# Weight conversions of an MLP's up stage tied to the relu, with a split first load and a reordered last norm

## The chip, the cores and the metric

The kernel runs on one core of a Trainium2 chip, as one launch. The metric is the device time of an execution in microseconds. The engines have short names here: PE (TensorE), DVE (VectorE), ACT (ScalarE), POOL (GpSimd) and SP (the queue that issues most DMAs).

## The reference

A decoder trunk of two layers on 512 tokens of width 1024, all in float32. Layer 0 is a gated short convolution, layer 1 a native sparse attention; each is followed by the same kind of MLP. The MLP is what most of this change is about.

```python
def rms_norm(x, g):
    y = x * lax.rsqrt(jnp.mean(x * x, axis=-1, keepdims=True) + EPS)
    return y * g

def squared_relu_mlp(h, w1, w2):              # w1 (1024, 4096), w2 (4096, 1024)
    return jnp.square(jax.nn.relu(h @ w1)) @ w2

def reference(x, ...):
    for layer in range(2):
        h = rms_norm(x, norm_mix[layer])
        x = x + (short_conv_mixer(h, ...) if layer == 0 else nsa_mixer(h, ..., shared, rel_bias))
        x = x + squared_relu_mlp(rms_norm(x, norm_mlp[layer]), mlp_w1[layer], mlp_w2[layer])
        if layer == 0:
            shared = nsa_shared_kv(rms_norm(x, kv_norm), ...)
    return rms_norm(x, final_norm)
```

## The kernel before

Products are made in float16 with three matmuls each (`mm3`): a float32 operand is split into a high half `hi` (ACT) and the remainder `lo` (DVE), and hi·hi, hi·lo and lo·hi are summed in PSUM. So every weight must be loaded (SP), then converted: `whi` by ACT and `wlo` by DVE. The weights are a list `pieces` in the order of use. Each has one of two kinds.

- An ordinary piece is [128, 1024] float32. Its tile is `wst` (`NS` = 3 buffers), its halves are `whi` and `wlo` (`NW` = 4).
- A block piece belongs to the down product. That product is made with seven block products instead of eight (a Strassen-Winograd scheme): DVE first adds four sums of 256-element blocks to the piece (line 180), then ACT writes `whi2` (line 182) and DVE `wlo2` (line 183), 1792 wide. There are three buffers for loading (`NS2`) and four for the halves (`NW2`), in the memory of the stage's own pool, so they can't be loaded before that pool opens.

`load_piece` issues the DMAs of the next piece, `convert_piece` converts the next one and loads another, `next_piece` hands the next one to a product, and `ahead` converts up to two ordinary pieces (`AHEAD`) or three block pieces (`AHEAD2`) ahead of use. One position in the list serves both kinds for each of these steps.

The program is written in a framework that places the instructions of each engine by a simulated schedule: an instruction may stand in its queue ahead of those that the text has before it, if its inputs are ready sooner. `tc.issue_after(ins)` keeps what is written in its block behind `ins` in the queue of the engine of `ins`, and does not bind other engines.

Each MLP runs in two halves of the hidden width: `mlp_up` on eight pairs of hidden tiles (p = 0 to 7), `mlp_down` on the result. A pair takes two pieces and 48 matmuls into two of six PSUM banks (lines 339 to 341). Then for each p: DVE scales and clips (`ml_t`, line 497), ACT squares (`ml_z`, 499), POOL adds four block sums (501), ACT writes `rh` (502) and DVE `rl` (503). `mlp_down` goes over four column blocks p; in each it runs over eight hidden tiles c with 21 matmuls each (lines 548 to 550), a block piece for two tiles. `ss.rstd` (lines 296 to 303) computes the reciprocal root of the norm ahead, during the first pair, and `broadcast_rows` (310) turns it into a row on PE.

The start: `x` comes in column chunks; PE transposes chunk c (line 372), ACT and DVE write its halves `x0h`, `x0l` with the norm's gain `vec`, which itself is a PE transpose (277) and two ACT copies (278, 279). `keep_busy` issues matmuls on zeros (237). The first eight weight pieces hold the three parts B, C and u of the mixer's input product side by side, 256 columns each.

The end: `last_b` finishes the last column block. Its combine steps are on DVE (1168), PE turns the result to token order (1121), ACT sums squares (1117), DVE multiplies by the gains (1192, 1198), and `store` computes the reciprocal root for two token tiles, scales them on ACT and DVE (1150 to 1157) and stores them (1158).

Of the kernel before, what the change touches and what calls it, by code (L numbers as in the profile page):

```python
# [48 lines left out]
def body(ctx, tc, x, rel_bias, norm_mix, norm_mlp, mlp_w1, mlp_w2, a_w_in, a_conv_w, a_w_out,  # L49
         kv_norm, w_kv, cmp_pe_k, cmp_pe_v, phi_k_w1, phi_k_w2, phi_v_w1, phi_v_w2,  # L50
         b_w_qg, b_w_o, final_norm, ident_c, onehot_c, out):
    nc = tc.nc
# [84 lines left out]
    W_SUMS = ((OP.add, 4, 0, 2), (OP.subtract, 5, 4, 1), (OP.subtract, 6, 1, 0), (OP.subtract, 7, 3, 5))  # L137
    R_SUMS = ((OP.subtract, 4, 0, 1), (OP.subtract, 5, 2, 4), (OP.subtract, 6, 2, 0), (OP.subtract, 7, 3, 5))

    PRODUCTS = ((1, 1), (3, 3), (5, 5), (6, 6), (4, 4), (7, 2), (2, 7))  # L140
    staged, ready = {}, {}
    pos = {"dma": 0, "cv": 0, "use": 0}
# [4 lines left out]
    def load_piece():  # L147
        i = pos["dma"]
        if i >= len(pieces):
            return  # L150
# [16 lines left out]
        pos["dma"] += 1  # L167

    def convert_piece(step=1024):

        i = pos["cv"]
        if i >= len(pieces):
            return
        _, shape, sc = pieces[i]
        t = staged.pop(i)
        pos["cv"] += 1
        if shape is None:
            b = t.rearrange("p (k b n) -> p k b n", k=2, n=128)
            for e, o, x, y in W_SUMS:
                DVE.tensor_tensor(b[:, :, o], b[:, :, x], b[:, :, y], op=e)  # L180
# [5 lines left out]
        else:  # L186
# [3 lines left out]
            for s in range(0, a * n, step):  # L190
                e = min(s + step, a * n)
                w = t[:, s:e]
                ACT.activation(hi[:, s:e], w, AF.Copy, scale=sc)  # L193
                DVE.scalar_tensor_tensor(lo[:, s:e], w, sc, hi[:, s:e], op0=OP.mult, op1=OP.subtract)  # L194
# [3 lines left out]
        while pos["dma"] < len(pieces):  # L198
            like = [j for j in range(pos["cv"], pos["dma"]) if blocked(j) == blocked(pos["dma"])]
            if len(like) >= (NS2 if blocked(pos["dma"]) else NS):  # L200
                break
            load_piece()

    def next_piece():

        i = pos["use"]
        pos["use"] += 1
        while i not in ready:
            for _ in convert_piece():
                pass  # L210
# [66 lines left out]
    PE.transpose(pv[:, 0:64], vec_in, ident[0:64, 0:64])  # L277
# [13 lines left out]

    def rstd_of(ss):
# [3 lines left out]
        ACT.activation(r, ss, AF.Sqrt, bias=eps, scale=1.0 / D)  # L296
# [46 lines left out]
    def pair(xs, ps, kn=8, mid=None):  # L343

        for c in range(kn):
            if c % 4 == 0:
                if c:
# [21 lines left out]
    def x_chunk(c):  # L369
# [3 lines left out]
        if c == 0:  # L373
            with tc.issue_after(last.ins):
# [110 lines left out]
    def mlp_up(xs, ss, rh, half, rb):  # L485
        turn[0] = 1
        for p in range(8):
            ph = [acc(), acc()]
            first = p == 0 and half == 0
            pair(xs, ph, mid=ss.rstd if first else None)  # L490
# [3 lines left out]
            drain(ahead())  # L494
            t = wk[0].tile([128, 2, S], F32, name="ml_t", bufs=1)
            for m in range(2):
                DVE.scalar_tensor_tensor(t[:, m], ph[m], 0.0, rb, op0=OP.max, op1=OP.mult)  # L497
# [76 lines left out]
    def first_half(hp, xs, ss):  # L574
        rh = tuple(hp.tile([128, 8, 7, 256], F16, name=n) for n in ("rh", "rl"))
# [22 lines left out]
    with pool("attn") as ap:  # L598
# [70 lines left out]
        def ahead_fine():  # L669
            while pos["cv"] < min(pos["use"] + AHEAD, len(pieces)):  # L670
                yield from convert_piece(512)
# [428 lines left out]
    with pool("hidden_b") as hp:  # L1100
# [42 lines left out]
        def store(h, late=None):  # L1143
            sst = work.tile([128, 2], F32, name="sst", bufs=2)
            DVE.tensor_reduce(sst, ssf[:, 2 * h:2 * h + 2], axis=mybir.AxisListType.X, op=OP.add)
            r = rstd_of(sst)
            for i in range(2):
                t = 2 * h + i
                a, b = xt[t][:, 0:512], xt[t][:, 512:1024]
                ACT.activation(a, a, AF.Copy, scale=r[:, i:i + 1])  # L1150
                if late:
                    b = xt[t][:, 512:768]
                    DVE.scalar_tensor_tensor(xt[t][:, 768:896], late[i], r[:, i:i + 1], gains(3, 1),
                                             op0=OP.mult, op1=OP.mult)
                    c = xt[t][:, 896:1024]
                    DVE.tensor_scalar(c, c, r[:, i:i + 1], None, op0=OP.mult)
                DVE.tensor_scalar(b, b, r[:, i:i + 1], None, op0=OP.mult)
                nc.sync.dma_start(out[0, t * 128:(t + 1) * 128, :], xt[t])

        def last_b(acc7, product):  # L1160
# [26 lines left out]
            stt(X1[:, n1], P2, X1[:, n1])  # L1187
            for t in range(2):
# [3 lines left out]
                DVE.tensor_tensor(xt[t][:, 768:1024], ps[:, 0:256], gains(3), op=OP.mult)  # L1192
            store(0)
            for t in range(2, 4):
# [3 lines left out]
                DVE.tensor_tensor(xt[t][:, 896:1024], ps[:, 0:128], gains(3)[:, 128:256], op=OP.mult)  # L1198
            product(6)
            stt(X2[:, n1], P4, X2[:, n1])  # L1200
# [6 lines left out]
            store(1, late)  # L1207
# [31 lines left out]
```

## Time and profile before

| what | value |
|---|---|
| timed runs | 1150.41, 1153.44, 1153.8 us; median 1153.44 |
| profiled execution | 1151.28 us, span 1149.5 us |
| mean granted PE clock | 0.994 |
| busy: PE, DVE, ACT, POOL | 1106.0, 837.8, 582.7, 162.2 us |
| DMA | 115.76 MB, mean 101 GB/s |

In a line of the timeline stand start, duration, engine, line of the kernel, operation, written and read tiles with shapes, and count; in brackets the idle time of the engine ahead of it and what ended it. A line of the waits has total, times and longest. A line of the stretches has the busy time of PE, PE's weight load, DVE, ACT and POOL, each with the number of instructions, then granted clock, DMA share and GB/s. Matmuls overlap; a 512-wide one is shown as 0.38 us and a 256-wide one as 0.27 us, whatever the distance to the next.

### The profile page before, as it was taken

The numbers are of one execution on the slowest core, as the hardware profiler recorded it, in microseconds if no ns is written. First come the engines' busy times: TensorE is split into PE (matmuls) and PEld (weight loads), VectorE is DVE, ScalarE is ACT, GpSimd is POOL, SyncE is SP. The second block draws the span as 40 slices with busy tenths as digits, with TensorE's granted clock in tenths as the row PEclk, the third lists the DMA queues.
The fourth block names the chain that finished last, engine by engine and source line by source line (L and its number), as shares of the span: only waits on it lengthen the run. The fifth ranks groups of instructions, "written<-read, shape, count | busy, mean of one in ns | idle before, by whom it ended". The sixth has DMA issues, their size and how long they took to land.

```text
span 1149.5 us, 20386 instructions
## 1 busy us (share of the span) xinstructions
PE 1106.0 (96%) x7959; PEld 694.1 (60%) x7959; DVE 837.8 (73%) x1604; ACT 582.7 (51%) x983; POOL 162.2 (14%) x211
## 2 busy tenths in 40 slices
PE   9999999999999999999999899999999999999996
PEld 4444444447884458868466665765444688445885
DVE  4755557765897557988487898997985588754795
ACT  4523235345333444457679778676644534343452
POOL 0000000422000220000120023111132200022031
PEclk9999999999999999999999999999999999999998
DMA  6433235433433333314333530111643343330231
GB/s 208 130 92 110 92 111 174 119 93 93 127 98 108 109 110 107 97 55 122 110 79 99 143 94 19 57 38 38 186 126 99 88 126 110 104 99 19 75 92 74
DMA packets 149379, 115.76 MB, mean 101 GB/s; under 512 B 8612, under 2 KB 146564, under 8 KB 149284
## 3 DMA queue, kind: packets, MB, share of 16 engines
q1 hardware_dynamic: 146736, 109.47, 31.8%
q10 hardware_dynamic: 2260, 4.40, 1.3%
q8 instruction: 62, 1.02, 0.4%
q0 software_dynamic: 288, 0.61, 0.2%
q14 instruction: 33, 0.27, 0.1%
HBM read 110.22 MB, written 2.14 MB: 98 GB/s over the span
## 4 chain that ended last, share of the span: by engine, by line
PE 49%; DVE 20%; ACT 12%; issue 8%; POOL 6%; DMA 4%; SPq 0%; DVEq 0%; ACTq 0%; POOLq 0%
POOL ml_z L501 6%; PE a L340 4%; PE a L339 4%; PE a L341 4%; DVE wlo L183 4%; DMA wst<-mlp_w_dram 4%; ACT rh L502 3%; PE b L339 3%; PE b L340 3%; PE b L341 3%; PE c L341 3%; PE c L339 3%; PE c L340 3%; DVE wst L180 3%; DVE wlo L194 3%
## 5 line engine op out<-in xcount | busy, mean ns | idle before, releaser
L193 ACT ACTIVATE whi<-wst 128x1024 f16<-128x1024 f32 (+2 forms) x171 | 142.2, 857 | 128.3 <-PE b L340 40.0
L194 DVE SCALAR_TENSOR_TENSOR wlo<-wst,whi 128x1024 f16<-128x1024 f32 (+2 forms) x171 | 168.1, 990 | 47.3 <-ACT whi L193 47.1
L501 POOL TENSOR_TENSOR ml_z<-ml_z 128x256 f32<-128x256 f32 x128 | 101.1, 811 | 604.5 <-ACT ml_z L499 403.9
L182 ACT ACTIVATE whi<-wst 128x1792 f16<-128x1792 f32 x64 | 107.0, 1692 | 132.6 <-DVE wst L180 107.8
L341 PEld LDWEIGHTS <-wlo 128*128 128x128 f16 x1024 | 100.1, 98 | 109.3 <-DVE wlo L194 0.7
L339 PEld LDWEIGHTS <-whi 128*128 128x128 f16 x1024 | 100.4, 98 | 108.1 <-issue 3.7
L503 DVE TENSOR_TENSOR rl<-ml_z,rh 128x1792 f16<-128x1792 f32 x32 | 64.8, 2025 | 136.9 <-ACT rh L502 136.9
L340 PEld LDWEIGHTS <-whi 128*128 128x128 f16 x1024 | 100.2, 98 | 105.0 <-issue 1.7
L183 DVE SCALAR_TENSOR_TENSOR wlo<-wst,whi 128x1792 f16<-128x1792 f32 x64 | 129.8, 2033 | 3.6 <-ACT whi L182 3.6
L180 DVE TENSOR_TENSOR wst<-wst 128x256 f32<-128x256 f32 x256 | 105.9, 455 | 24.1 <-DMA wst<-mlp_w_dram 23.1
L502 ACT ACTIVATE rh<-ml_z 128x1792 f16<-128x1792 f32 x32 | 54.3, 1697 | 103.4 <-POOL ml_z L501 103.4
L550 PEld LDWEIGHTS <-wlo 128*128 128x128 f16 x896 | 88.1, 98 | 16.6 <-issue 5.1
L549 PEld LDWEIGHTS <-whi 128*128 128x128 f16 x896 | 88.1, 98 | 14.8 <-issue 3.9
L548 PEld LDWEIGHTS <-whi 128*128 128x128 f16 x896 | 88.2, 98 | 11.0
L499 ACT ACTIVATE ml_z<-ml_t 128x1024 f32<-128x1024 f32 x32 | 33.8, 1057 | 90.5 <-DVE ml_t L497 90.5
L341 PE MATMUL b<-xsh,wlo 128*128 128x512 f16 x208 | 78.8, 379 | 0.0
L340 PE MATMUL b<-xsl,whi 128*128 128x512 f16 x208 | 78.8, 379 | 0.0
L339 PE MATMUL b<-xsh,whi 128*128 128x512 f16 x208 | 78.7, 379 | 0.0
L922 ACT ACTIVATE at_p<-at_s,at_m 128x128 f32<-128x128 f32 (+3 forms) x128 | 71.3, 557 | 13.4 <-DVE at_m L919 13.0
L549 PE MATMUL a<-rl,whi 128*128 128x256 f16 x256 | 70.3, 275 | 4.6 <-DVE rl L503 4.6
L339 PE MATMUL c<-xsh,whi 128*128 128x512 f16 x192 | 72.8, 379 | 0.0
L340 PE MATMUL c<-xsl,whi 128*128 128x512 f16 x192 | 72.8, 379 | 0.0
(312 smaller groups left out, 2757.5 us busy)
## 6 DMA issues: line engine op xcount, KB each, us to landing
wst<-mlp_w_dram SPq DMA_DIRECT2D x256, 256.0 KB, 3.4
wst<-a_w_in_dram SPq DMA_DIRECT2D x18, 512.0 KB, 3.6
wst<-w_kv_dram SPq DMA_DIRECT2D x12, 512.0 KB, 3.7
T<-ext_d ACTq DMA_DIRECT2D x4, 1056.0 KB, 6.0
wst<-a_w_out_dram SPq DMA_DIRECT2D x8, 512.0 KB, 3.5
wst<-b_w_qg_dram SPq DMA_DIRECT2D x8, 512.0 KB, 4.3
wst<-b_w_o_dram SPq DMA_DIRECT2D x8, 512.0 KB, 3.5
wst<-a_w_in_dram SPq DMA_DIRECT2D x8, 384.0 KB, 5.5
```

The source lines that it names most:

```text
L180: DVE.tensor_tensor(b[:, :, o], b[:, :, x], b[:, :, y], op=e)
L182: ACT.activation(hi, b[:, :, 1:], AF.Copy, scale=sc)
L183: DVE.scalar_tensor_tensor(lo, b[:, :, 1:], sc, hi, op0=OP.mult, op1=OP.subtract)
L193: ACT.activation(hi[:, s:e], w, AF.Copy, scale=sc)
L194: DVE.scalar_tensor_tensor(lo[:, s:e], w, sc, hi[:, s:e], op0=OP.mult, op1=OP.subtract)
L339: PE.matmul(ps, w[0], xs[0], start=start, stop=False)
L340: PE.matmul(ps, w[0], xs[1], start=False, stop=False)
L341: PE.matmul(ps, w[1], xs[0], start=False, stop=stop)
L501: POOL.tensor_tensor(z[:, o], z[:, a], z[:, b], op=e)
L502: ACT.activation(rh[0][:, p], z[:, 1:8], AF.Copy)
L548: PE.matmul(acc7[i], wh, xh, start=c == 0 and not other, stop=False, skip_group_check=other)
L549: PE.matmul(acc7[i], wh, xl, start=False, stop=False, skip_group_check=other)
```

## The change

1. The one list position becomes one queue for each kind (`to_load`, `to_convert`), with `fill(kind)` to load as long as buffers are free; `layer_end` keeps block pieces of the next layer out.
2. In `mlp_up` the products no longer call `ahead`. At p = 0 block pieces begin to load and two ordinary pieces are converted. Behind the scaled relu (`issue_after(done.ins)`) come two ordinary pieces for p below 6, and one block piece for p = 1 to 4.
3. Two of the four block sums become one instruction over two blocks.
4. The first piece is loaded and converted in three parts, and the idle matmuls of the start are put behind the turn of `vec` as well.
5. In the last norm the gain multiplies and both reciprocal roots go behind the last combine step; token tile 0 is scaled on POOL, tile 1 on ACT, and the stores stand in the order 0, 2, 3, 1.

```diff
-    def load_piece():
-        i = pos["dma"]
...
+    def load_piece(kind=False):
+        i = to_load[kind].pop(0)
...
+            elif i == 0:
+                for part in FIRST_PARTS:
+                    nc.sync.dma_start(v[:, part], src[:, part])
...
+    def fill(kind):
+        while (to_load[kind] and sum(blocked(j) == kind for j in staged) < (NS2 if kind else NS)
+               and not (kind and to_load[kind][0] > layer_end[0])):
+            load_piece(kind)
...
-            for e, o, x, y in W_SUMS:
-                DVE.tensor_tensor(b[:, :, o], b[:, :, x], b[:, :, y], op=e)
+            DVE.tensor_tensor(b[:, :, 4], b[:, :, 0], b[:, :, 2], op=OP.add)
+            DVE.tensor_tensor(b[:, :, 5:7], b[:, :, 4:0:-3], b[:, :, 1::-1], op=OP.subtract)
+            DVE.tensor_tensor(b[:, :, 7], b[:, :, 3], b[:, :, 5], op=OP.subtract)
...
+            if i == 0:
+                spans = [(n * part, n * part + n) for part in FIRST_PARTS]
...
     def ahead():
-        while pos["cv"] < len(pieces) and pos["cv"] < pos["use"] + (AHEAD2 if blocked(pos["cv"]) else AHEAD):
-            yield from convert_piece()
+        for kind in (False, True):
+            while to_convert[kind] and to_convert[kind][0] < use[0] + (AHEAD2 if kind else AHEAD):
+                yield from convert_piece(kind)
...
-            with tc.issue_after(last.ins):
+            with tc.issue_after(last.ins), tc.issue_after(vec_turn.ins):
                 keep_busy(5)
...
-            pair(xs, ph, mid=ss.rstd if first else None)
+            pair(xs, ph, mid=ss.rstd if first else None, convert=False)
...
-            drain(ahead())
+            if p == 0:
+                fill(True)
+                for _ in range(2):
+                    drain(convert_piece(False))
...
-                DVE.scalar_tensor_tensor(t[:, m], ph[m], 0.0, rb, op0=OP.max, op1=OP.mult)
+                done = DVE.scalar_tensor_tensor(t[:, m], ph[m], 0.0, rb, op0=OP.max, op1=OP.mult)
+
+            with tc.issue_after(done.ins):
+                if p < 6:
+                    for _ in range(2):
+                        drain(convert_piece(False))
+                if 1 <= p < 5:
+                    drain(convert_piece(True))
...
     def first_half(hp, xs, ss):
+        layer_end[0] = use[0] + 63
...
-            store(1, late)
+            with tc.issue_after(final.ins):
+                for t, ps, at, g in early:
+                    DVE.tensor_tensor(xt[t][:, at], ps, g, op=OP.mult)
+                r = stats(0)
+                lo, hi = slice(0, 512), slice(512, 1024)
+                for at in (lo, hi):
+                    v = xt[0][:, at]
+                    POOL.tensor_tensor(v, v, r[:, 0:1].to_broadcast([128, 512]), op=OP.mult)
+                put(0)
+                r1 = stats(1)
+            with tc.issue_after(rstd_root[0].ins):
+                ACT.activation(xt[1][:, lo], xt[1][:, lo], AF.Copy, scale=r[:, 1:2])
+                for i in range(2):
+                    v = xt[2 + i][:, lo]
+                    ACT.activation(v, v, AF.Copy, scale=r1[:, i:i + 1])
+                    DVE.scalar_tensor_tensor(xt[2 + i][:, 768:896], late[i], r1[:, i:i + 1], gains(3, 1),
+                                             op0=OP.mult, op1=OP.mult)
+                    v = xt[2 + i][:, 896:1024]
+                    DVE.tensor_scalar(v, v, r1[:, i:i + 1], None, op0=OP.mult)
+                    v = xt[2 + i][:, 512:768]
+                    DVE.tensor_scalar(v, v, r1[:, i:i + 1], None, op0=OP.mult)
+                    put(2 + i)
+                ACT.activation(xt[1][:, hi], xt[1][:, hi], AF.Copy, scale=r[:, 1:2])
+                put(1)
```

`final` is the last combine step (line 1168 before), `stats` returns the reciprocal root of two token tiles, `put(t)` stores one, and `rstd_root[0]` is the latest square root on ACT.

More of the change, by code (lines that the diff above doesn't have):

```diff
@@ L276, in body @@
     pv = bank("e")
[L277 removed]
+    vec_turn = PE.transpose(pv[:, 0:64], vec_in, ident[0:64, 0:64])
     ACT.activation(vec[:, 0:40], pv[:, 0:40], AF.Copy, scale=SX)
@@ L669, in ahead_fine @@
         def ahead_fine():
-            while pos["cv"] < min(pos["use"] + AHEAD, len(pieces)):
-                yield from convert_piece(512)
+            while to_convert[False] and to_convert[False][0] < use[0] + AHEAD:
+                yield from convert_piece(False, 512)
         def keys(br):
@@ L1141, in done_b, with stats, put @@
             yield
-        def store(h, late=None):
+        def stats(h):
             sst = work.tile([128, 2], F32, name="sst", bufs=2)
             DVE.tensor_reduce(sst, ssf[:, 2 * h:2 * h + 2], axis=mybir.AxisListType.X, op=OP.add)
[L1146 to L1158, printed above, removed]
+            return rstd_of(sst)
+        def put(t):
+            nc.sync.dma_start(out[0, t * 128:(t + 1) * 128, :], xt[t])
         def last_b(acc7, product):
@@ L1191, in last_b @@
                 square(ps[:, 0:256], t, 3)
-                DVE.tensor_tensor(xt[t][:, 768:1024], ps[:, 0:256], gains(3), op=OP.mult)
-            store(0)
+                early.append((t, ps[:, 0:256], slice(768, 1024), gains(3)))
             for t in range(2, 4):
```

47 lines of the change are left out of this document (21 added, 26 removed).

## The prediction

> **What bounds the kernel now.** I read the engine totals first, then what the matmul queue waited for, then the timeline of the few places found.
>
> ```profile
> PE 1106.0 (96%) x7959; PEld 694.1 (60%) x7959; DVE 837.8 (73%) x1604; ACT 582.7 (51%) x983; POOL 162.2 (14%) x211
> ...
> 855.00:885.00 30.00, 30.00 (x140) 13.50 (x139) 18.66 (x22) 13.63 (x12) 10.40 (x12) 1.00 0.36 105
> ```
>
> TensorE is the bound. Inside the up stage it never rests: 140 matmuls in 30.00 us are 0.214 us each, so one pair (48 matmuls) takes 10.3 us. A change that removes no matmul can give back only pauses, half-clock time and the two ends. The waits of TensorE say which pauses belong to the MLP stages and the tail:
>
> ```profile
> PE a L549 <- DVE rl L503: 4.6, 3, 1.8
> PE e L310 <- DVE rs_r L303: 1.8, 2, 1.4
> PE c L1121 <- DVE X L1168: 1.4, 1, 1.4
> PE a L548 <- ACT rh L502: 1.0, 1, 1.0
> ...
> 284.85 0.27 PE L549 MATMUL a<-rl,whi 128*128 128x256 f16 x1 [1.55 <-DVE rl L503]
> 442.48 0.27 PE L549 MATMUL a<-rl,whi 128*128 128x256 f16 x1 [1.23 <-DVE rl L503]
> 913.78 0.27 PE L548 MATMUL a<-rh,whi 128*128 128x256 f16 x1 [1.05 <-ACT rh L502]
> 915.84 0.37 PE L549 MATMUL a<-rl,whi 128*128 128x256 f16 x1 [1.79 <-DVE rl L503]
> ...
> 915.90:921.60 5.70, 5.70 (x28) 4.04 (x28) 3.76 (x2) 2.85 (x3) 0.00 (x0) 0.50 0.34 99
> 921.60:930.00 8.40, 8.40 (x78) 7.49 (x77) 8.17 (x14) 1.70 (x1) 0.00 (x0) 0.99 0.39 123
> ```
>
> Three of the four up halves end in a pause: the down stage has used seven of the eight hidden tiles and waits for the last one's `rh`/`rl`. After the third pause the granted clock is 0.50 for 5.7 us: 28 matmuls where 53 would have fitted (78 in 8.40 us are 0.108 each).
>
> Why the last `rl` is late is in the DVE queue of the same half:
>
> ```profile
> 265.47 1.28 DVE L497 SCALAR_TENSOR_TENSOR ml_t<-b,rb 128x512 f32<-128x512 f32 x2
> 266.67 1.21 DVE L194 SCALAR_TENSOR_TENSOR wlo<-wst,whi 128x1024 f16<-128x1024 f32 x1
> 272.58 2.02 DVE L503 TENSOR_TENSOR rl<-ml_z,rh 128x1792 f16<-128x1792 f32 x1 [4.70 <-ACT rh L502]
> 274.52 1.22 DVE L194 SCALAR_TENSOR_TENSOR wlo<-wst,whi 128x1024 f16<-128x1024 f32 x1
> 275.66 1.28 DVE L497 SCALAR_TENSOR_TENSOR ml_t<-c,rb 128x512 f32<-128x512 f32 x2
> 282.77 2.03 DVE L503 TENSOR_TENSOR rl<-ml_z,rh 128x1792 f16<-128x1792 f32 x1 [4.70 <-ACT rh L502]
> ```
>
> This is a serial loop: relu, square on ACT, four sums on POOL, `rh` on ACT, `rl` on DVE, a weight's `wlo`, next relu. It turns in 10.19 us (265.47 to 275.66), hardly faster than the 10.3 us of a pair, so a lag once caught is never made up. PSUM holds three pairs, so TensorE runs ahead and pays only at the end. The lag is caught early, when block sums and their `wlo` are run greedily:
>
> ```profile
> 211.11 1.28 DVE L497 SCALAR_TENSOR_TENSOR ml_t<-c,rb 128x512 f32<-128x512 f32 x2
> 212.31 1.21 DVE L194 SCALAR_TENSOR_TENSOR wlo<-wst,whi 128x1024 f16<-128x1024 f32 x1
> 213.44 2.02 DVE L183 SCALAR_TENSOR_TENSOR wlo<-wst,whi 128x1792 f16<-128x1792 f32 x1
> 215.37 2.68 DVE L180 TENSOR_TENSOR wst<-wst 128x256 f32<-128x256 f32 x3
> 220.40 2.02 DVE L503 TENSOR_TENSOR rl<-ml_z,rh 128x1792 f16<-128x1792 f32 x1 [2.35 <-ACT rh L502]
> ...
> 224.15 1.28 DVE L497 SCALAR_TENSOR_TENSOR ml_t<-a,rb 128x512 f32<-128x512 f32 x2
> ```
>
> That turn took 13.04 us.
>
> **The change, part by part.** The sum is made against the profiled execution, 1151.28 us (span 1149.5 and 1.8 around it). The timed runs are 1150.41, 1153.44 and 1153.8; the mean of all four is 1152.2, and I put the saving on that.
>
> *Pins in the up stage.* No work is removed. After each relu come two `wlo` of the pair two ahead (p below 6) and, for p = 1 to 4, one block piece; for p = 6 and 7 nothing. So `rl` is followed directly by the next relu. A turn without a block becomes 10.19 - 1.14 (274.52 to 275.66) = 9.05 us, 1.25 under a pair: lag is now made up. A turn with a block is nearest to the row of 211.11: relu to the end of `rl` is 9.29 + 1.94 = 11.2 us, with one `wlo`, one block `wlo` and three sums inside and 2.35 us idle, which takes the second `wlo` (1.13) and the fourth sum. So 0.9 us over a pair, 3.6 us after four, made up by p = 7. The last `rl` then ends about 9 us after the last up matmul, while seven hidden tiles (147 matmuls of 0.108, 15.9 us) cover it. If that cover were short, the old pauses return. All three pauses go. The idle figures start at a modelled end, 0.27 after the start, where the pace is 0.108, so each stands for 0.16 more: 5.62 + 0.64 = 6.26 us, and the half clock 5.70 - 28 x 0.108 = 2.7 us. Together 8.9 us; bounds 3 (only the lag of the third half goes) and 9.
>
> One rule of the Trainium skill bears on the 2.7 us: "TensorE: Matmul & The Clock Gate", Part 1, has the clock halved only after an idle window of about 3.4 us. By that rule of the Trainium skill pauses of 1.05 and 1.79 us would not have done it; the rows show 0.50 right behind them, and I go by the rows.
>
> *Waits that are added.* Behind a pinned `wlo` in DVE's queue wait block sums, `rl` and the next relu. TensorE needs the `wlo` of pair p+2 when that pair starts, 10.3 us after pair p; they end 1.2 + 2 x 1.2 = 3.6 us after the relu begins. The cover is 6.7 us of lag.
>
> *Loads.* Two queues of pieces replace one, and SP gets the first three block loads at p = 0.
>
> ```profile
> wst<-mlp_w_dram SPq DMA_DIRECT2D x256, 256.0 KB, 3.4
> ```
>
> What is queued behind them on SP are the up pieces, two DMAs each; three are staged and two are used per 10.3 us, so 3.4 us to landing leaves slack of about 3 us behind `wlo`. I cost this at nothing, up to 3 us once if the cover is gone.
>
> *The norm before the up stage.*
>
> ```profile
> 191.32 0.17 DVE L299 RECIPROCAL rs_r<-rs_r 128x4 f32<-128x4 f32 x1
> 191.40 1.99 DVE L183 SCALAR_TENSOR_TENSOR wlo<-wst,whi 128x1792 f16<-128x1792 f32 x1
> 193.31 0.15 DVE L301 TENSOR_TENSOR rs_t<-rs_r 128x4 f32<-128x4 f32 x1
> 194.20 1.08 DVE L180 TENSOR_TENSOR wst<-wst 128x256 f32<-128x256 f32 x3
> ```
>
> A block's `wlo` and two sums sit inside the chain of the reciprocal root. With block pieces pinned behind p = 1 they cannot. The two waits (1.8 us above) go: 1.7 us, bounds 0 (an up `wlo` takes the place) and 2.
>
> *Two sums in one.* Three 256-element sums take 1.08 us, 0.34 each; two 512-element relus start 0.60 apart. So 2 x 0.34 - 0.60 = 0.08 us per piece, 5 us over 64 pieces, all beside TensorE: 0 on the path, bounds 0 and -0.6.
>
> *First piece by parts; idle matmuls behind the gain turn.*
>
> ```profile
> 5.67 1.89 PE L237 MATMUL c<-idle 128*128 128x512 f16 x5
> 7.49 0.28 PE L277 MATMUL e<-ident,vec_in 64*128 64x64 f32 x1
> 8.45 0.66 PE L372 MATMUL e<-ident,xt 128*128 128x128 f32 x4 [0.68 <-ACT vec L279]
> 9.09 0.38 PE L339 MATMUL a<-x0h,whi 128*128 128x512 f16 x1
> ```
>
> The turn moves ahead of five idle matmuls (1.8 us), so the gains and the first `x0h` come that much sooner, and a third of the piece lands and converts first. If the first product still follows chunk 1's transposes, which wait for that chunk's load, 0.3 us is won; if not, it starts at about 7.7, 1.4 us sooner. I take 0.8.
>
> *Last norm.*
>
> ```profile
> 1138.16 0.27 PE L550 MATMUL e<-rh,wlo 128*128 128x256 f16 x1
> ...
> 1139.42 0.40 DVE L1168 SCALAR_TENSOR_TENSOR X<-e,X 128x256 f32<-128x256 f32 x1
> 1141.31 0.96 SPq L1158 DMA_DIRECT2D out_dram<-xsh  x2
> 1144.37 1.05 SPq L1158 DMA_DIRECT2D out_dram<-xsl  x2
> ...
> 1142.20:1144.60 2.40, 0.00 (x0) 0.00 (x0) 2.07 (x11) 1.33 (x3) 0.00 (x0) 0.79 1.00 399
> out_dram<-xsl SPq DMA_DIRECT2D x2, 512.0 KB, 2.9
> L739 POOL TENSOR_TENSOR Q<-at_s,Q 64x512 f16<-64x512 f32 x16 | 19.2, 1197 | 72.7 <-ACT Q L738 71.8
> ```
>
> The last combine step can start at about 1138.5 instead of 1139.42: 0.9 us. But tiles 0 and 1, stored from 1141.31 until now, wait for work that is put behind it, and all four stores come in one bunch. A store is 0.52 MB, 1.3 us at 399 GB/s, and the row of 2.9 us leaves 1.6 us around that. Before, the last bunch of two landed at about 1144.37 + 1.6 + 2.6 = 1148.6. After, the first store is the question. If a tile of the second pair goes first: 1144.37 stands 4.95 us behind the combine step, from 1138.5 that is 1143.4, less one 512-wide scaling on ACT that no longer stands ahead of the squares, about 1142.7 (an estimate). If tile 0 goes first and the others queue behind it on SP: the gain multiplies that are now behind the step hold the first root until about 1141.5, and POOL's two multiplies at 1.2 us each, with some contention, end near 1144.2. With 1.6 + 5.2 us behind it the last landing is 1149.5 or 1151.0: a loss of 0.9 to 2.4 us. I take 1.5.
>
> Sum: -8.9 - 1.7 - 0.8 + 1.5 = -9.9 us: 1152.2 - 9.9 = 1142.3 (1141.4 beside the profiled execution).
>
> **Rivals.**
> *The pauses come back elsewhere* (the last hidden tile stays late, or the scheduled order hardly differs, so that the change does not do what it says). For: the loop through ACT and POOL stays. Against: the fourth half has no such wait and no pause. Then only 1.0 us is left: 1151.2.
>
> *The clock drop is not the pause's.* Then the 2.7 us stay: 1145.0. For it: the clock rule of the Trainium skill named above. Against: the two shorter pauses kept the clock, this pair lost it.
>
> *DVE's loop becomes the bound, the slower side.* Place: turns p = 1 to 4 of each half. It decides from a turn of 10.3 + 6.7/4 = 12.0 us, where the `wlo` of pair p+2 come late. At the 13.04 us measured above, 4 x 2.7 - 6.7 = 4.1 us per half, 17 us in all: 1159; one more us per turn gives 1175. For it: three sums took 2.68 us beside POOL's and 1.08 us alone. The Trainium skill agrees ("GPSIMD Engine Reference", 8. Key points): GpSimd and VectorE contend for SBUF when a VectorE instruction has two SBUF inputs, and the pin puts just those beside POOL's sums. Against: the row of 13.04 holds a `wlo` and two sums behind `rl`, with 2.35 us idle ahead of it.
>
> **How the numbers follow.** Forecast 0.64 (own range 1138.5 to 1147), clock rival 0.12, pauses rival 0.12, DVE loop 0.12. About 0.3% (3.5 us) is what a measurement of this kernel can tell from no change. Faster: forecast and clock rival, 0.76, and a little of the pauses rival, 0.77; same 0.12; slower 0.11. The range 1138 to 1151.5 leaves out the DVE loop and the edges.
>
> **What would show it.** Right: no wait of L549 for `rl` at the up ends, granted clock 1.00 there, `rl` directly before a relu, turns under 12 us for p = 1 to 4, no block `wlo` inside the root's chain, the first L339 before 9.0, the last store landing over 10 us after the last L550. Wrong: TensorE idle in the up stage before `whi`/`wlo` of a new pair, or idle at hidden tile eight.

## The result and the profile after

The changed kernel takes 1166.08 us (median of six runs, 1164.76 to 1169.35); beside it the kernel before took 1152.8. The ratio is 1.012, 95% interval 1.0095 to 1.0145: 13 us slower, where 10 us faster was forecast. The profiled execution took 1169.14 us (span 1167.4), so it is 3 us above its median, and the profiled one of before 1.5 us below: the two traces differ by 17.9 us of span, the medians by 13.3.

The engine totals of the changed kernel, and its waits of TensorE that bear on the change:

```profile
PE 1114.4 (95%) x7959; PEld 697.8 (60%) x7959; DVE 862.3 (74%) x1540; ACT 583.5 (50%) x985; POOL 188.9 (16%) x213
```
```profile
PE c L349 <- DVE wlo L204: 8.2, 4, 2.7
...
PE a L567 <- DVE rl L521: 4.2, 3, 1.8
...
PE a L566 <- ACT xsh L1151: 2.9, 1, 2.9
```

POOL, given no new work in the up stage, is busy 27 us longer: 24 us of it in its block sums (101.1 before, 125.3 now), 2 in the last norm. TensorE has a wait that it did not have, in the up stage, for `wlo`; most of the old wait for `rl` at the start of the down products is still there (L549 before, L567 now); the wait for the reciprocal root (L310 before, 1.8 us) is gone. Why `wlo` comes late stands in the timeline (DVE, ACT, POOL, PE and SP together; the last six rows are the last matmul and the last norm):

```profile
217.41 1.28 DVE L508 SCALAR_TENSOR_TENSOR ml_t<-a,rb 128x512 f32<-128x512 f32 x2
218.61 2.35 DVE L204 SCALAR_TENSOR_TENSOR wlo<-wst,whi 128x1024 f16<-128x1024 f32 x2
219.86 4.54 POOL L519 TENSOR_TENSOR ml_z<-ml_z 128x256 f32<-128x256 f32 x4 [8.09 <-ACT ml_z L517]
220.88 0.95 DVE L186 TENSOR_TENSOR wst<-wst 128x256 f32<-128x256 f32 x1
221.86 1.09 DVE L187 TENSOR_TENSOR wst<-wst 128x512 f32<-128x512 f32 x1
222.99 0.83 DVE L188 TENSOR_TENSOR wst<-wst 128x256 f32<-128x256 f32 x1
224.44 1.70 ACT L520 ACTIVATE rh<-ml_z 128x1792 f16<-128x1792 f32 x1 [4.65 <-POOL ml_z L519]
226.04 1.68 ACT L190 ACTIVATE whi<-wst 128x1792 f16<-128x1792 f32 x1
226.17 2.03 DVE L521 TENSOR_TENSOR rl<-ml_z,rh 128x1792 f16<-128x1792 f32 x1 [2.35 <-ACT rh L520]
228.11 2.02 DVE L191 SCALAR_TENSOR_TENSOR wlo<-wst,whi 128x1792 f16<-128x1792 f32 x1
230.05 1.28 DVE L508 SCALAR_TENSOR_TENSOR ml_t<-b,rb 128x512 f32<-128x512 f32 x2
...
256.51 1.28 DVE L508 SCALAR_TENSOR_TENSOR ml_t<-a,rb 128x512 f32<-128x512 f32 x2
257.71 2.35 DVE L204 SCALAR_TENSOR_TENSOR wlo<-wst,whi 128x1024 f16<-128x1024 f32 x2
258.98 0.39 PE L349 MATMUL c<-xsh,wlo 128*128 128x512 f16 x1 [2.67 <-DVE wlo L204]
...
1154.40 0.27 PE L568 MATMUL e<-rh,wlo 128*128 128x256 f16 x1
1154.71 0.42 DVE L1210 SCALAR_TENSOR_TENSOR X<-e,X 128x256 f32<-128x256 f32 x1 [1.62 <-PE e L568]
...
1157.59 2.04 POOL L1224 TENSOR_TENSOR xsh<-xsh,rs_r 128x512 f32<-128x512 f32 x2 [10.74 <-DVE rs_t L310]
1159.65 0.36 SPq L1168 DMA_DIRECT2D out_dram<-xsh  x1
1160.11 1.21 SPq L1168 DMA_DIRECT2D out_dram<-xsl  x2
1161.41 1.14 SPq L1168 DMA_DIRECT2D out_dram<-xsh  x1
```

In the kernel before, a turn in which DVE was idle beside POOL's sums had this row:

```profile
237.36 2.90 POOL L501 TENSOR_TENSOR ml_z<-ml_z 128x256 f32<-128x256 f32 x4 [7.29 <-ACT ml_z L499]
```

A turn from relu to relu takes 12.64 us (217.41 to 230.05), and two things in it are new. POOL's four sums take 4.54 us beside `wlo` and the block sums, where they took 2.90 with DVE idle. And the block's `wlo` (L191) stands between `rl` and the next relu, because its `whi` (L190) stands behind `rh` in ACT's queue, and `rh` waits for POOL. The `wlo` of the last pair is pinned behind the relu at 256.51; TensorE waits 2.67 us for it.

Stretches of the changed kernel; the column behind the five engines is the granted clock:

```profile
259.00:262.50 3.50, 3.50 (x10) 1.26 (x11) 2.84 (x3) 0.00 (x0) 3.42 (x4) 0.55 0.90 272
...
600.00:610.00 10.00, 8.18 (x91) 6.67 (x89) 7.03 (x20) 8.05 (x21) 4.15 (x4) 0.83 0.31 90
640.00:650.00 10.00, 7.32 (x74) 5.28 (x74) 9.83 (x30) 7.31 (x23) 1.10 (x1) 0.83 0.60 169
800.00:810.00 10.00, 7.99 (x55) 3.59 (x52) 2.32 (x5) 0.89 (x2) 2.52 (x4) 0.83 0.16 52
...
927.00:932.00 5.00, 4.01 (x22) 2.97 (x22) 4.80 (x3) 3.90 (x4) 0.00 (x0) 0.66 0.11 31
...
1112.40:1117.00 4.60, 4.49 (x27) 3.20 (x27) 4.57 (x4) 3.15 (x8) 4.60 (x4) 0.63 0.36 116
```

Half clock follows the new pause at 258.98, the pause ahead of 927 and the 2.9 us wait for `xsh` in the last down product: (1 - clock) x length gives 1.6 + 1.7 + 1.7 = 5.0 us, against 2.7 us before. The three stretches between 600 and 810 lie in the attention layer, which the change doesn't touch: 1.7 us each that the profiled execution before did not lose: its granted clock is 1.00 from 6.97 to 914.91, the third pause.

What decides it can be read from the granted clock. In each of the 14 traces the spells of half clock (up to the end of the last matmul) last 3.41 us or twice that, and all of one trace begin on a grid with a step of 3.41 us; the grid lies elsewhere in most traces. A spell begins where TensorE was idle for some half of the step before. The first two rows are two steps of the changed kernel's grid; the last two are the kernel before at the same matmuls:

```profile
600.67:604.09 3.42, 1.60 (x21) 0.97 (x17) 2.48 (x5) 3.01 (x7) 3.27 (x3) 1.00 0.00 0
604.09:607.50 3.41, 3.41 (x28) 3.01 (x27) 2.92 (x11) 2.10 (x6) 0.28 (x1) 0.50 0.28 77
```
```profile
595.27:598.68 3.41, 1.59 (x21) 0.96 (x17) 2.46 (x5) 3.02 (x7) 3.26 (x3) 1.00 0.00 0
598.68:602.09 3.41, 3.41 (x51) 3.03 (x51) 3.41 (x14) 2.70 (x8) 0.30 (x1) 1.00 0.22 60
```

The same 21 matmuls leave the same 1.82 us idle in both; at the other two places it is 1.76 and 2.01 us, in both as well. In the trace before these are cut by edges of its grid (the first at 597.50), and no step of its attention layer has more than 1.59 us idle. So these 5.1 us come from where the grid lies and not from a longer wait; without them the spans differ by 12.8 us, near the medians. What sets the grid's place in an execution stays open.

So the last matmul, 16.2 us later in this pair of traces, is: waits for `wlo` +8.7 (8.2, and one of 0.5 in another PSUM bank), half clock in the MLP stages +2.3, attention +5.1, the wait for `xsh` +2.1 (2.9 instead of 0.8), waits for `rl` and `rh` -1.0 (4.6 instead of 5.6), the norm roots -2.1, the start +0.6; together 15.7. The last norm adds 1.6.

### The profile page after: what moved, and what is told of

It reads as the page before. It is cut to its first block, busy times and chain, and to the rows that moved or that the text cites. A ratio compares the mean times of both kernels' runs of the same rounds, so it can differ in the third digit from the quotient of the medians.

```text
span 1167.4 us, 20258 instructions
## 1 busy us (share of the span) xinstructions
PE 1114.4 (95%) x7959; PEld 697.8 (60%) x7959; DVE 862.3 (74%) x1540; ACT 583.5 (50%) x985; POOL 188.9 (16%) x213
## 4 chain that ended last, share of the span: by engine, by line
PE 62%; DVE 13%; ACT 10%; POOL 6%; issue 6%; DMA 1%; SPq 0%; DVEq 0%; ACTq 0%; POOLq 0%
POOL ml_z L519 6%; PE a L348 5%; PE a L347 5%; PE a L349 5%; PE b L347 4%; PE b L348 4%; PE b L349 4%; PE c L349 3%; PE c L348 3%; PE c L347 3%; PE c L947 2%; DVE ml_t L508 2%; ACT rh L520 2%; DVE wlo L191 2%; PE c L566 2%
## 5 line engine op out<-in xcount | busy, mean ns | idle before, releaser
L519 POOL TENSOR_TENSOR ml_z<-ml_z 128x256 f32<-128x256 f32 x128 | 125.3, 999 | 593.4 <-ACT ml_z L517 590.9
L203 ACT ACTIVATE whi<-wst 128x1024 f16<-128x1024 f32 (+3 forms) x173 | 143.3, 849 | 152.2 <-PE b L348 55.9
L204 DVE SCALAR_TENSOR_TENSOR wlo<-wst,whi 128x1024 f16<-128x1024 f32 (+3 forms) x173 | 166.2, 979 | 46.9 <-ACT whi L203 46.8
L190 ACT ACTIVATE whi<-wst 128x1792 f16<-128x1792 f32 x64 | 106.8, 1688 | 102.9 <-DVE wst L188 79.3
L191 DVE SCALAR_TENSOR_TENSOR wlo<-wst,whi 128x1792 f16<-128x1792 f32 x64 | 130.0, 2036 | 4.6 <-ACT whi L190 4.0
L567 PEld LDWEIGHTS <-whi 128*128 128x128 f16 x896 | 88.1, 98 | 16.4 <-issue 5.4
L566 PEld LDWEIGHTS <-whi 128*128 128x128 f16 x896 | 88.2, 98 | 11.1
L349 PE MATMUL c<-xsh,wlo 128*128 128x512 f16 x192 | 73.5, 383 | 8.2 <-DVE wlo L204 8.2
L567 PE MATMUL a<-rl,whi 128*128 128x256 f16 x256 | 70.6, 276 | 4.2 <-DVE rl L521 4.2
L566 PE MATMUL a<-rh,whi 128*128 128x256 f16 x256 | 70.4, 275 | 3.5 <-ACT xsh L1151 2.9
L938 DVE CUSTOM_DVE_ANT_0 at_s<-b,T 128x128 f32<-128x128 f32 (+3 forms) x128 | 61.1, 481 | 17.1 <-PE b L934 6.4
```

Of the source, the lines that this page charges most:

```text
L190: ACT.activation(hi, b[:, :, 1:], AF.Copy, scale=sc)
L191: DVE.scalar_tensor_tensor(lo, b[:, :, 1:], sc, hi, op0=OP.mult, op1=OP.subtract)
L349: PE.matmul(ps, w[1], xs[0], start=False, stop=stop)
L519: POOL.tensor_tensor(z[:, o], z[:, a], z[:, b], op=e)
L566: PE.matmul(acc7[i], wh, xh, start=c == 0 and not other, stop=False, skip_group_check=other)
L567: PE.matmul(acc7[i], wh, xl, start=False, stop=False, skip_group_check=other)
```

## The experiments

A turn is the distance between the first relu instructions of two pairs. Turns are of the first half, p = 0 to 6; "sums" is the mean of POOL's L519 (one 256-wide sum, 128 of them); "waits" is TensorE in the up stages for `wlo`. Ratios are against the kernel before, run beside each.

| kernel | median us | ratio, 95% | turns, us | sums, ns | waits, us |
|---|---|---|---|---|---|
| before | 1152.8 | | 12.49 13.04 10.77 10.19 10.19 10.18 10.19 | 811 | 0 |
| changed | 1166.08 | 1.012, 1.0095 to 1.0145 | 10.02 12.65 12.63 13.23 13.23 11.65 10.19 | 999 | 8.7 |
| block outside the pin | 1157.49 | 1.0039, 1.0024 to 1.0054 | 10.44 12.03 10.98 10.00 10.00 11.14 10.18 | 956 | 4.8 |
| halves a turn later | 1179.63 | 1.0232, 1.021 to 1.0254 | 10.01 10.70 12.77 14.96 14.03 14.16 10.18 | 1101 | 18.3 |
| `rl` a turn later | 1189.83 | 1.0317, 1.0298 to 1.0336 | 8.80 14.25 14.23 14.24 14.23 12.18 10.80 | 1244 | 30.3 |
| before, `rl` a turn later | 1168.03 | 1.013, 1.0108 to 1.0151 | 6.28 19.01 11.29 10.80 10.80 10.80 10.80 | 1159 | 1.2 |
| one input | 1139.48, one run | | 9.11 11.84 11.84 11.39 11.52 10.24 10.18 | 797 | 0 |
| before, start and last norm | 1157.13 | 1.0033, 1.0017 to 1.0049 | 12.47 13.03 10.77 10.18 10.18 10.18 10.18 | 808 | 0 |
| loop apart | 1140.98 | 0.99, 0.9869 to 0.9931 | 9.02 10.36 10.80 10.75 12.25 11.88 11.31 | 1285 | 0 |
| loop apart, old last norm | 1139.71 | 0.9881, 0.9857 to 0.9905 | 9.02 10.36 10.81 10.74 12.26 11.88 11.31 | 1286 | 0 |
| four sums | 1174.15 | 1.0183, 1.0158 to 1.0207 | 10.03 12.38 12.37 13.38 14.63 12.33 10.19 | 1032 | 13.6 |
| ACT's order alone | 1163.47 | 1.0092, 1.0066 to 1.0118 | 10.98 11.12 11.16 11.15 14.63 13.19 11.88 | 1085 | 11.9 |
| nothing ahead | 1172.67 | 1.0185, 1.0165 to 1.0205 | 10.02 12.64 12.63 12.63 12.64 10.02 9.05 | 990 | 5.3 |
| ACT's order, nothing ahead | 1151.5 | 0.9999, 0.9981 to 1.0017 | 10.97 11.11 11.15 11.14 11.15 10.94 9.04 | 1099 | 0 |

**Block piece outside the pin**

```diff
-                if 1 <= p < 5:
-                    drain(convert_piece(True))
+            if 1 <= p < 5:
+                drain(convert_piece(True))
```

> The changed kernel with the block piece of p = 1 to 4 written outside the pin (the ordinary pieces stay pinned). Theory (the pinned block piece makes DVE's turn longer than a pair: turns of 12.6 to 13.2 us, then TensorE waits 2.67 + 1.44 + 0.48 + 2.70 + 1.42 us for a pinned `wlo`): the schedule may place the block's steps in idle time, turns fall to about 11 us, the waits of L349 for `wlo` go (8.2 to under 2 us), and the time falls by 5 to 10 us, to 1156 to 1161. Rival (the loss sits in other places: attention +4.7, last down product +3.3, tail +1.6, start +0.65 us by the shift of the matmuls): less than 3 us come back, 1163 or more.

8.6 us came back, within what the theory gave; the turns are mostly 10 to 12 us. Of the 4.8 us of waits left (under 2 were expected), 1.8 come in the third half, whose first two turns take 13.72 and 14.83. The other 3.0 come early in the second and fourth half, for the `wlo` of the third pair: they are pinned behind the first relu, and in the second half that relu starts 10.6 us after its pair is done, because block sums stand ahead of it and one of them waits 2.12 us for its load. TensorE waits for the reciprocal root again, 3.0 us. So the pinned block is the largest part of the loss and not all of it.

**Halves of a block a turn later**

```diff
             DVE.tensor_tensor(b[:, :, 7], b[:, :, 3], b[:, :, 5], op=OP.subtract)
+            yield
...
+                drain(halves)
...
-                    drain(convert_piece(True))
+                    halves = convert_piece(True)
+                    next(halves)
```

> The changed kernel with a block's sums pinned behind relu p as before, but its `whi2` and `wlo2` behind relu p+1. Theory (the 1.94 us of the block `wlo` stand between `rl` and the next relu, because its `whi2` on ACT comes behind `rh`): the block `wlo` moves into the 2.35 us that DVE idles ahead of `rl`, turns fall from 12.6 to 10.7 us, the waits of L349 for `wlo` go, the pauses at the start of the down products shrink from 4.2 us to under 2; 1154 to 1159. Rival (POOL's four sums, 4.55 us beside the pinned two-input operations instead of 2.9, are what holds the turn, and the block `wlo` only follows them): turns stay above 12 us and the time above 1163.

A miss: only the second turn is the 10.7 of the theory. From the next one on `wlo2` stands right behind the relu and pushes both `wlo` into POOL's time; the sums of further pieces come on top (turns to 14.96).

**`rl` a turn later, in the changed kernel and in the one before**

```diff
+                if p:
+                    q, y = late
+                    DVE.tensor_tensor(rh[1][:, q], y[:, 1:8], rh[0][:, q], op=OP.subtract)
...
-            DVE.tensor_tensor(rh[1][:, p], z[:, 1:8], rh[0][:, p], op=OP.subtract)
+            late = (p, z)
...
```

> The changed kernel with the subtract `rl` of pair p pinned behind the relu of pair p+1, so that DVE no longer waits in a turn for POOL and ACT. Theory (a turn is a serial loop through ACT and POOL, not DVE's own work): DVE's own work per turn is 1.3 + 1.9 + 2.4 + 2.7 + 1.9 = 10.2 us with a block and 5.6 without, so relu follows the pair, TensorE never waits for `wlo` in the up stage, no pause at the start of the down products and no half clock behind them; what is left against the kernel before is attention, last down product, tail and start: 1146 to 1155. Rival (the sum of DVE's work is the bound): turns with a block stay above 12 us, 1160 or more.

> The kernel before with the same deferral of `rl` alone. Theory (the old pauses come from the same serial loop): the waits of the first down products for `rl` (4.6 us) and `rh` (1.0 us) and the half clock behind the third go, 6.3 + 2.7 = 8.9 us: 1143 to 1146. Rival (the lag is DVE's greedy order ahead of the relu, not the loop): the pauses stay, 1150 to 1155. Third reading (the half clock is not the pause's): 1146 to 1148.

Both far off, and slower. From one turn of the first of them, ACT and DVE:

```profile
226.21 1.70 ACT L523 ACTIVATE rh<-ml_z 128x1792 f16<-128x1792 f32 x1 [5.66 <-POOL ml_z L522]
227.82 1.04 ACT L203 ACTIVATE whi<-wst 128x1024 f16<-128x1024 f32 x1
228.76 1.68 ACT L190 ACTIVATE whi<-wst 128x1792 f16<-128x1792 f32 x1
...
230.47 2.03 DVE L191 SCALAR_TENSOR_TENSOR wlo<-wst,whi 128x1792 f16<-128x1792 f32 x1 [3.29 <-ACT whi L190]
232.42 0.68 DVE L508 SCALAR_TENSOR_TENSOR ml_t<-b,rb 128x512 f32<-128x512 f32 x1
```

`rl` is out of the way, but the loop is still closed, through ACT: the relu waits for the block's `wlo`, that for its `whi`, that for `rh` ahead of it in ACT's queue, and `rh` for POOL's sums, now 5.55 us because `rl` runs beside them as well. In the kernel before it is the same with the ordinary `whi`: DVE waits 4.78 us in each turn of 10.80.

**`wlo` behind the relu with one SBUF input** (the subtraction is left out)

```diff
-                DVE.scalar_tensor_tensor(lo[:, s:e], w, sc, hi[:, s:e], op0=OP.mult, op1=OP.subtract)
+                if one_input[0]:
+                    DVE.tensor_scalar(lo[:, s:e], w, sc / 2048, None, op0=OP.mult)
...
```

> The changed kernel with the ordinary `wlo` behind the relu written as a product with a constant: one SBUF input instead of two. Left out: the subtraction of `whi` there, so the remainder is not the reference's. Theory (a DVE instruction with two SBUF inputs and POOL's sums hold each other up): POOL's sums beside those `wlo` go from 1.68 to 0.72 us each, the four sums of a block turn from 4.55 to 3.3 to 3.9 us (the block sums beside them keep two inputs), those of p = 0 from 3.80 to 2.9; turns with a block from 12.64 to 11.4 to 12.0. Rival (POOL is slowed by any DVE instruction beside it, or by ACT): the four sums stay at 4.5 us and the turn at 12.6, less only what the `wlo` themselves get shorter.

The four sums of a block turn fall from 4.55 to 3.75, those of p = 0 from 3.80 to 2.89, and the turn with a block by the same 0.8, to 11.84. That is enough for all waits and all pauses to go: 1139.48 in its one run. But the form also takes 0.68 us instead of 1.22, so both `wlo` are over before POOL starts. The run shows that what overlaps POOL's sums sets the turn; it doesn't show that a single input by itself would have left POOL alone.

**Start and last norm alone, on the kernel before**

> The kernel before with two parts of the change alone: the start (first piece by parts, idle matmuls behind the gain turn) and the last norm. By the forecast's steps: the last store lands 11.1 to 12.6 us after the last matmul instead of 10.17, and the first product starts at 8.3 instead of 9.09. By the trace of the changed kernel: 11.8 us after the last matmul, first product at 9.3. Time 1152.8 + 1.6 and -0.8 to +0.7: 1153.6 to 1155. Rival (these two ends carry most of the 13 us lost): 1158 or more.

The edits are parts 4 and 5 of the change as listed. The last store lands 11.80 us after the last matmul begins, against 10.17 before; it is 11.78 to 11.81 in every version that has the new last norm and 10.14 to 10.17 in those with the old: 1.64 us lost. The first product starts at 8.09 here, but at 7.79 to 9.65 over the versions with the new start and at 8.69 and 9.09 with the old: not resolved. The ratio says 3.8 us slower (2.0 to 5.6), 2 more than expected. Its trace has a wait of 1.84 us for `xsh` in the last down product and four spells of half clock in attention; the cause of these 2 us stays open.

**The loop taken apart on both engines**

```diff
+            square = ACT.activation(z[:, 0:4].rearrange("p (m k) n -> p m (k n)", m=2), t, AF.Square)
+            with tc.issue_after(done.ins), tc.issue_after(square.ins):
+                if p:
+                    q, y = late
+                    DVE.tensor_tensor(rh[1][:, q], y[:, 1:8], rh[0][:, q], op=OP.subtract)
...
+                drain(halves)
                 if 1 <= p < 5:
-                    drain(convert_piece(True))
+                    halves = convert_piece(True)
+                    next(halves)
...
+            with tc.issue_after(last_hi[0].ins):
+                ACT.activation(rh[0][:, p], z[:, 1:8], AF.Copy)
```

> The changed kernel with the up stage's loop taken apart on both engines: `rl` of pair p behind the relu of pair p+1 (DVE), the `whi` of a turn and the `whi2` of the block before behind the square and ahead of `rh` (ACT), `wlo2` of a block one turn later. Theory (the earlier deferral of `rl` failed because `wlo` and `wlo2` still waited for an ACT step behind `rh`, so the loop stayed closed through ACT): nothing in DVE's queue waits for POOL any more, DVE's own work is 8.8 us a turn with a block, 10 to 11 with POOL beside it; no wait of L350 for `wlo`, no wait for `rl` at the start of a down product, no half clock behind it: 1152.8 - 8.9 - 1.6 (root) + 1.6 (tail) + up to 3 us from elsewhere, 1143 to 1148. Rival (DVE's and POOL's work together is the bound, since they hold each other up): turns with a block stay above 12 us and TensorE goes on waiting for `wlo`, 1158 or more.

> The same with the last norm of the kernel before. Theory: 1.6 us less than its twin, 1141.5 to 1146.5, the last store landing 10.2 us after the last matmul. Rival (the longer tail is an accident of one execution): equal to its twin within 0.7 us.

Both are faster than either kernel: 1140.98 and 1139.71 us, a little below the ranges given. One turn of the first:

```profile
223.47 1.27 DVE L510 SCALAR_TENSOR_TENSOR ml_t<-b,rb 128x512 f32<-128x512 f32 x2
224.66 2.01 DVE L518 TENSOR_TENSOR rl<-ml_z,rh 128x1792 f16<-128x1792 f32 x1
225.91 5.56 POOL L529 TENSOR_TENSOR ml_z<-ml_z 128x256 f32<-128x256 f32 x4 [5.19 <-ACT ml_z L513]
226.59 0.95 DVE L187 TENSOR_TENSOR wst<-wst 128x256 f32<-128x256 f32 x1
227.47 3.41 DVE L206 SCALAR_TENSOR_TENSOR wlo<-wst,whi 128x1024 f16<-128x1024 f32 x2
230.81 1.21 DVE L188 TENSOR_TENSOR wst<-wst 128x512 f32<-128x512 f32 x1
231.50 1.70 ACT L531 ACTIVATE rh<-ml_z 128x1792 f16<-128x1792 f32 x1 [2.19 <-POOL ml_z L529]
231.94 2.01 DVE L193 SCALAR_TENSOR_TENSOR wlo<-wst,whi 128x1792 f16<-128x1792 f32 x1
233.87 0.41 DVE L189 TENSOR_TENSOR wst<-wst 128x256 f32<-128x256 f32 x1
234.21 1.27 DVE L510 SCALAR_TENSOR_TENSOR ml_t<-c,rb 128x512 f32<-128x512 f32 x2
```

No DVE row has an idle time: DVE waits for nobody. POOL's sums are the slowest of all versions (1285 ns in the mean, four in 5.56 us) and it costs nothing, because `rh` is wanted a turn later. TensorE has no wait for `wlo`, `rl` or `rh`. Against the kernel before its matmuls come forward by 1.72, 1.39 and 6.02 us around the three starts of down products. The old last norm is worth 1.3 us by the medians; the intervals of the two overlap, and the landing (10.14 against 11.79) is the better witness.

**Four block sums again, in the changed kernel**

```diff
-            DVE.tensor_tensor(b[:, :, 5:7], b[:, :, 4:0:-3], b[:, :, 1::-1], op=OP.subtract)
+            DVE.tensor_tensor(b[:, :, 5], b[:, :, 4], b[:, :, 1], op=OP.subtract)
+            DVE.tensor_tensor(b[:, :, 6], b[:, :, 1], b[:, :, 0], op=OP.subtract)
```

> The changed kernel with four block sums instead of three (part 3 taken back). By the forecast: 0 on the path, 0 to 0.6 us. Theory (the turn is the sum of relu, square, POOL's sums, `rh`, `rl`, `wlo2`, and what is beside POOL's sums lengthens them): a turn with a block gets longer by 0.0 to 0.3 us, four of them in each half all behind the point where TensorE waits for `wlo`, so 0 to 4.8 us slower than the changed kernel, 1166 to 1171. Rival (two 256-wide sums are lighter on POOL than one of 512): up to 3 us faster, 1163.

8 us slower than the changed kernel, above the range. A plain block turn is 0.26 us shorter, as the rival had it (12.38, four sums of POOL in 4.28). But the schedule puts the sums of two pieces into one turn at p = 4, which takes 14.63, and there POOL's first sum takes 3.36 us:

```profile
242.68 2.35 DVE L205 SCALAR_TENSOR_TENSOR wlo<-wst,whi 128x1024 f16<-128x1024 f32 x2
243.93 3.36 POOL L520 TENSOR_TENSOR ml_z<-ml_z 128x256 f32<-128x256 f32 x1 [9.10 <-ACT ml_z L518]
...
246.29 0.42 DVE L189 TENSOR_TENSOR wst<-wst 128x256 f32<-128x256 f32 x1
```

**ACT's order alone** (the version with the loop apart, `rl` in its own turn again)

> The version with the loop taken apart, but with `rl` of pair p again in its own turn: ACT's order alone (`whi`, and `whi2` of the block before, ahead of `rh`). Theory: `wlo2` goes from its place between `rl` and the relu into the time in which DVE waited, but beside POOL; a turn is relu and square 2.4, POOL 5.5, `rh` 1.7, `rl` 1.94: 11.6 us instead of 12.6 to 13.2, just under the 12.0 from which TensorE waits for `wlo`: under 1 us of those waits, pauses at the start of the down products as in the kernel before, 1146 to 1152. Rival (the deferral of `rl` does nothing, ACT's order is all): as the version with both, 1140 to 1143. Rival (ACT's order does nothing, the deferral is all): 1160 or more, as in the changed kernel.

Four turns of 11.1 us, a little under the 11.6 worked out, and then a row that no theory had:

```profile
237.54 0.68 DVE L510 SCALAR_TENSOR_TENSOR ml_t<-c,rb 128x512 f32<-128x512 f32 x1
240.74 0.42 DVE L187 TENSOR_TENSOR wst<-wst 128x256 f32<-128x256 f32 x1 [2.53 <-DMA wst<-mlp_w_dram]
241.08 0.68 DVE L510 SCALAR_TENSOR_TENSOR ml_t<-c,rb 128x512 f32<-128x512 f32 x1
```

The simulated schedule has placed the first sum of a down-stage piece between the two halves of a relu; DVE waits 2.53 us for its load, and the second half of the relu waits behind it. So the miss could come from such work pulled ahead or from the missing deferral of `rl`, which the last two runs were to tell apart. In this version and in the second of the next two `wlo2` still comes a turn later, so ACT's order is not quite alone.

**Nothing pulled ahead**

```diff
+    behind = [None]
...
     def drain(gen):
-        for _ in gen:
-            pass
+        if behind[0]:
+            with tc.issue_after(behind[0].ins):
+                for _ in gen:
+                    pass
...
+            rl = DVE.tensor_tensor(rh[1][:, p], z[:, 1:8], rh[0][:, p], op=OP.subtract)
+        behind[0] = rl
```

> The changed kernel in which what is written behind a half's last `rl` also stands behind it on DVE: no step of the down stage or of the next half may be pulled ahead into the up stage. Theory (part of the late turns is such work: the sums of a second piece at p = 3 and 4, two `wlo` at p = 6 and 7): turns 12.64 for p = 1 to 4, never 13.23, then 10.0 and 9.05; waits for `wlo` from 8.7 to about 2.5 us, the pauses for `rl` at the start of the down products (4.2 us) go, and half clock with them: 10 to 13 us less than the changed kernel, 1153 to 1156. Rival (the pulled-ahead work ran in time in which DVE would have waited): the same within 3 us, 1163 or more.

> ACT's order alone (`whi` and `whi2` ahead of `rh`), with nothing pulled ahead. In the run before it four turns took 11.15 us, as ACT's order should give, and then two took 14.6 and 13.2, with the sums of a down piece between the two halves of a relu, waiting 2.5 us for their load. Theory (that stray work made its 1163): turns 11.0 to 11.2 for p = 0 to 4 and about 10 and 9 behind them, no waits for `wlo`, no pauses: 1140 to 1145, as with `rl` deferred as well. Rival (without the deferral of `rl` the loop stays too slow): 1150 or more.

The turns came out nearly as stated in both. In the first the waits for `wlo` in the up stage fall from 8.7 to 5.3 and those for `rl` go, yet it is 6.6 us slower than the changed kernel. Its waits of TensorE say why:

```profile
PE c L576 <- DVE wlo L191: 9.3, 6, 2.2
...
PE c L356 <- DVE wlo L204: 4.0, 4, 2.1
PE c L574 <- ACT whi L190: 4.0, 3, 1.3
```

L574 and L576 are down products: 12.0 of these 13.3 us are at the fifth block piece of a down stage, which comes late in all four. What was pulled ahead was needed. The second run has no wait in the up stage and none for `rl`, so ACT's order does stop those waits without the deferral of `rl`; at 1151.5 it misses the 1140 to 1145 nevertheless, with 3.1 us of waits for block `wlo` in the down stage and 2.3 us for `xsh` plus half clock behind it. Which share is the missing deferral's, it doesn't say.

## Why the prediction was wrong, and where it was right

- **The step that failed: "A turn with a block ... 11.2 us", whose idle 2.35 us "takes the second `wlo` (1.13) and the fourth sum".** From relu to the end of `rl` it is 10.70 us (217.41 to 228.11), better than the row it was taken from. But that row had the block `wlo` of an earlier piece inside. In the changed kernel it is the same turn's, its `whi` stands behind `rh`, and so its 1.94 us come behind `rl` and ahead of the relu: 12.64. I looked at DVE's queue for the place of `wlo` and not at ACT's for the `whi` that it needs. The sums of further pieces made two turns 13.23. Two versions of the changed kernel with all turns under 12.0 us have no wait for `wlo` in the up stage: 11.90 at most with the shorter `wlo` (one input), 11.16 with ACT's order and nothing pulled ahead. So the place of `whi` and the work beside POOL's sums made the long turn together, and relief on either ended those waits.
- **"Made up by p = 7" failed as well.** The turn of p = 0, with two `wlo` and no block, takes 10.02 and not 9.05, because POOL's sums beside them take 3.80 us. The last turns are 11.65 and 10.19, not 9.05: the schedule fills p = 5 to 7 with sums and `wlo` of what comes next. When this was forbidden the turns were 10.02 and 9.05, but the down stage waited. Lag and time ahead are paid from the same idle time.
- **The rival "DVE's loop becomes the bound" is what happened**, at the place it named. It put the cover at 6.7 us and the deciding turn at 12.0. Measured: in the first half five turns take 61.76 us, 10.26 more than five pairs of 10.3, and TensorE waits 2.67: a cover of 7.6. With nothing ahead the turns take 60.56, the lag is 9.06, the wait 1.46: 7.6 again. By the same sum the changed kernel's third half gives 6.6 and its second and fourth 9.2. Per half the waits are 1.4 to 3.2 us, less than its 4.1; the time is above its 1159 because old pauses stay (4.6 us) and half clock follows the new ones. Its reason, contention with POOL, holds: 2.90 to 4.55 us for four sums. As the Trainium skill says ("GPSIMD Engine Reference", 8. Key points), POOL contends with DVE instructions that have two SBUF inputs; the traces agree for `wlo`, block sums and `rl`, all of that kind. A relu reads one of its two inputs from PSUM: beside one (before, `rl` a turn later, at 1068.94) a sum took 0.72 us, as with DVE idle.
- **The price of the pauses, 8.9 us, was right.** With the loop apart 1.72 + 1.39 + 6.02 = 9.1 us come back, and the median is 1140.98 where 1142.3 was forecast, for an order that the change did not make.
- **Half clock is the pause's.** The rival on the clock falls: in the version without pauses there is none in the MLP stages. By the Trainium skill ("TensorE: Matmul & The Clock Gate", Part 1) it takes an idle window of about 3.4 us; here single pauses of 2.67 and 2.9 us were followed by 0.55 and 0.63. A pause of 1.44 us in the second half was followed by 1.00. Length alone does not decide: 1.79 us at 927.99, whole in one step of the grid with 0.37 us of idle time ahead of it, was followed by half clock; 1.79 us at 447.59 and 2.70 us at 899.41, each cut by an edge, were not. The prediction's pair of 1.05 and 1.79 us put 1.91 us into the step that ended at 914.91.
- **Norm roots:** forecast -1.7; the matmuls behind the two roots come forward by 1.54 and 0.61. **Last norm:** forecast +1.5, measured +1.64, by the mechanism given: the two multiplies of tile 0 on POOL (2.04 us) end at 1159.63, 5.2 us after the last matmul, and all four stores are issued behind that. **Start:** forecast -0.8, not resolved. **Two sums in one:** forecast 0; in this kernel it is worth about 8 us, because the turn is where the schedule's arrangement of sums decides. "All beside TensorE" was true of DVE's time and not of POOL's. **Loads:** no TensorE wait for one in the up stages.

## What to carry to other kernels

Before work is pinned into an engine's idle time, follow the loop that makes the idle time through all its engines: what the pinned step itself waits for in another queue, and which of them it slows by running beside them. A turn longer than the bound's own pace can be paid twice, once when the cover of buffers is gone and again in the clock behind the pause. What gained here with all the work done was opening the loop on both engines at once. Opened on DVE alone it was slower than either kernel's own order; opened on ACT, with `rl` left in its turn, it was slower than the kernel before (1163.47) or, with nothing pulled ahead, equal to it (1151.5).

## What the hardware showed that was not expected

- A 256-wide sum on POOL takes 0.72 us with DVE idle (2.90 for four). In the changed kernel the `wlo` at 219.74 keeps its 1.22 us, and the sum that starts 0.12 us behind it takes 1.68; in the version with the loop apart, where sums are already running, each of the two `wlo` takes 1.75 (1.22 alone). So the two nearly take turns, and the later one pays. It is not always shared: above, one sum took 3.36 us while DVE ran five sums behind the `wlo` at their undisturbed 0.42.
- Half clock came in spells of 3.41 us on a grid that lies elsewhere in most traces. Over all traces, behind the first 20 us, a step at full clock with less than 1.5 us of idle TensorE time never led to one and a step with more than 2.05 us always did; between the two both occur (idle times as the traces show them, with modelled ends). So the same instructions can lose 5.1 us in one execution and nothing in another. The mean granted clock of the timed runs of the kernel before goes from 0.990 to 0.997.
